# Two decoder layers on one core: which matmul a chain step, a norm's transposes and a broadcast are issued behind, and how eight PSUM banks are divided

## The chip, the cores and the metric

One core of one Trainium2 chip runs the whole program. The metric is device time in microseconds (us) of one execution; the median of the executions is compared. TensorE is PE in the profile, VectorE DVE, ScalarE ACT, GpSimd POOL and SyncE, which issues the weight loads, SP.

## What is computed

Two layers of a decoder trunk on 256 tokens of width 2048, in float32:

```python
for i in range(DEPTH):                                   # 2 layers
    h = h + mixers[i](rmsnorm(h, attn_norms[i]))         # 0: DeltaNet heads + latent attention, 1: retention
    h = h + conv_ffn(rmsnorm(h, ffn_norm), w_up, conv_w, conv_b, w_down)   # 2048 -> 2*5632 -> 2048
    h = h + (p[i] @ w_proj) * sigmoid(rmsnorm(h, gate_norm) @ w_gate)      # per-layer embedding (PLE)
return rmsnorm(h, final_norm)
```

In layer 0 the mixer projects the normed h with one 2048 x 5200 matrix. Eight gated DeltaNet heads get q, k, v and z from it. Each head needs a long chain of small products: normed keys, a triangular system solved by repeated products of 128 x 128 blocks, then the output. Eight latent-attention heads get low-rank queries and keys.

## The kernel before

**Projections.** Every weight is loaded from memory in pieces of up to 1 MB (`load`), and `split` makes of each piece a rounded part `hi` (a cast on ACT, L183) and a remainder `lo` (a subtraction on DVE, L184). Activations are kept in the same two parts. `gemm_b` computes 256 output columns transposed: for each half of the 2048 rows, sixteen `hi` matmuls of 512 columns (L239) and sixteen `lo` ones of 256 (L243). `gemm_a` computes up to 512 output columns for both halves of the tokens, with 8 + 8 `hi` matmuls (L265, L266) and 8 `lo` ones (L270) for each 512 rows of the weight. Both are Python generators: each `yield` is a place at which the program may put other work. `joined` reads a `gemm_b` result out of PSUM (ACT L249, DVE L250).

**Order of issue.** A scheduler goes through the program as it is written. On each engine it issues the earliest written instruction that its own model of the durations takes to be ready; the written order alone does not fix the order on PE. A NoSync edge (`tc.issue_after(x)`) keeps what is written in its block behind x on x's engine.

**The mixer of layer 0.** The heads go in four pairs. `Pair.solve` is the chain from the keys to the solved system `Ut`, `Pair.mix` the chain from there to the head's output, `masks` the decay factors that `solve` needs. Stage `step` of five runs `solve` of pair `step` and `mix` of pair `step - 1` in turns (`turns`). `weave(main, filler, rate)` writes `rate` pieces of filler after each step of a chain. The filler is the projections of the next heads (`gdn_gemm`) and the attention of one pair of heads (`mla`), alternating; in the last stage it is the output projection (`proj_add`). A piece of filler is some 1.4 to 1.9 us of matmuls, but four of the fifteen pieces of `mla` are empty. `unit_norm` transposes a head's keys or queries into a PSUM bank and returns that bank; it is read a second time after the norm is known (DVE L625 for k, L685 for q).

**Norms.** `Norm.feed(c)` transposes 512 columns of h on PE (`gained`, L285) and writes them in two parts (ACT L289, DVE L290). It is called as soon as `proj_add` has added its result to those columns (DVE L329). `Norm.finish` forms the factor of each token (DVE L311 and L312, a power on POOL in `rsqrt` L157) and, where it is asked to, turns it into a row with a diagonal (DVE L317), a matmul with ones (PE L319) and a copy (ACT L321). `low_rank` does the same for the low-rank queries and keys (DVE L481) and transposes at once.

**PSUM.** There are eight banks. Tiles `pa` take two banks, tiles `pb` one. The mixer of layer 0 has two `pa` and four `pb`; then this pool is closed and another with three `pa` and two `pb` opened for all that follows.

Of the kernel before, what the change touches and what calls it, by code (L numbers as in the profile page):

```python
# [29 lines left out]
PSUM0 = (2, 4)  # L30
PSUM1 = (3, 2)
NPART = 3
RATES = [2.0, 1.0, 1.0, 1.0, 2.5]
# [48 lines left out]
def trunk(ctx: ExitStack, tc: tile.TileContext, a: dict):  # L82
# [9 lines left out]
    banks = {}  # L92

    @contextmanager
    def psum(wide, narrow):

        with tc.tile_pool(name="psa", bufs=wide, space=PSUM) as banks["a"], tc.tile_pool(name="psb", bufs=narrow, space=PSUM) as banks["b"]:
            yield
# [17 lines left out]
    def pa():  # L116
        return banks["a"].tile([P, 2, 512], F32, tag="pa", name=nm("pa"))

    def pb():
        return banks["b"].tile([P, 512], F32, tag="pb", name=nm("pb"))  # L120
# [74 lines left out]

    def weave(main, filler, rate):
        owed = 0.0
        for _ in main:
            owed += rate
            while owed >= 1.0:  # L200
                owed -= 1.0
                next(filler, None)
        run(filler)
# [26 lines left out]
    def gemm_b(w, c0, tiles):  # L230
        ps = pa()
        for c in range(2):
            hi, lo = split(w[c * 1024 : (c + 1) * 1024, c0 : c0 + 256], 8, 256)
            for j in range(2):
                for k in range(8):
                    x2, xh = xr(tiles, c * 8 + k)
                    wh = hi[k][:, j * P : (j + 1) * P]
                    first = c == 0 and k == 0
                    T.matmul(ps[:, j], wh, x2, start=first, stop=False)  # L239
                yield  # L240
            for j in range(2):
                for k in range(8):
                    T.matmul(ps[:, j, :S], lo[k][:, j * P : (j + 1) * P], xr(tiles, c * 8 + k)[1], start=False, stop=c == 1 and k == 7)  # L243
# [11 lines left out]
    def gemm_a(w, r0, nkb, c0, n, tiles, ps=None, begin=True, end=True):  # L255
        if ps is None:
            ps = pa()
        k0 = 0
        while k0 < nkb:
            nk = min(4, nkb - k0)  # L260
            hi, lo = split(w[r0 + k0 * P : r0 + (k0 + nk) * P, c0 : c0 + n], nk, n)
            for i in range(NH):
                for k in range(nk):
                    xh, xw = xl(tiles, k0 + k, i)
                    T.matmul(ps[:, i, :n], xh, hi[k], start=begin and k0 + k == 0, stop=False)  # L265
                    T.matmul(ps[:, i, :n], xw, hi[k], start=False, stop=False)  # L266
                yield
            for i in range(NH):
                for k in range(nk):
                    T.matmul(ps[:, i, :n], xl(tiles, k0 + k, i)[0], lo[k], start=False, stop=end and k0 + k == nkb - 1)  # L270
# [23 lines left out]
    class Norm:  # L294
# [14 lines left out]
        def finish(self, bc):  # L309
# [5 lines left out]
            if bc:  # L315
                dg = t1((P, 2, P))
                V.tensor_tensor(dg, bcm(ident, 2), bcs(self.r, P), op=ALU.mult)  # L317
                ps = pb()
                T.matmul(ps[:, :S], ones, dg.rearrange("p a b -> p (a b)"), start=True, stop=True)  # L319
                self.bc = cp.tile([P, S], F32, name=nm("rbc"), tag="rbc")  # L320
                A.copy(self.bc, ps[:, :S])  # L321

    def proj_add(w, parts, cols, after=None):
        for c in cols:
# [5 lines left out]
            if after is not None:  # L330
                after(c)
# [44 lines left out]
    layer0 = ExitStack()  # L376
    layer0.enter_context(psum(*PSUM0))

# [18 lines left out]
    for c in range(CG):  # L397
        if c < CG - 2:
            for i in range(NH):
                load_x(i, c + 2)  # L400
        for _ in range(2):
            next(first_gemm)
        if c < CG - 1:
            n0.feed(c + 1)
        with tc.issue_after(last_gain[0].ins):
            Norm.squares(n0, c)
        next(first_gemm)
    n0.finish(True)
# [64 lines left out]
    def low_rank(src, gain):  # L473
# [8 lines left out]
        return gained(src, gain)  # L482

    for g3 in range(3):
# [7 lines left out]
        if g3 == 2:  # L492
            gates()
            cqT = low_rank(cq, C_QN)
# [88 lines left out]
    def unit_norm(f):  # L583
        ps = units(f)
        sq = t2((P, 4, P))
        A.activation(sq, v4(ps), AF.Square)
# [5 lines left out]
        return ps, rr  # L592

    class Pair:
# [27 lines left out]
        def solve(self):  # L622
            ps, rk = unit_norm(box.pop((self.hp, 1)))
            kh = self.kh = t2((P, 4, P))
            V.tensor_tensor(kh, v4(ps), bcs(rk, P), op=ALU.mult)  # L625
            yield from self.masks()
# [54 lines left out]
        def mix(self):  # L681
            hp, kh, kT, Ut = self.hp, self.kh, self.kT, self.Ut
            ps, rq = unit_norm(box.pop((hp, 0)))
            qh = t2((P, 4, P))
            V.scalar_tensor_tensor(qh, v4(ps), P ** -0.5, bcs(rq, P), op0=ALU.mult, op1=ALU.mult)  # L685
# [3 lines left out]
            V.tensor_tensor(vb, v4(ps), bcs(self.sc(beta), P), op=ALU.mult)  # L689
            yield  # L690
# [4 lines left out]
            ps = mm2(Ut, vb, first, first)  # L695
            u0 = t1((P, 2, P))
            A.copy(u0, two(ps))
            kd = t1((P, 2, P))
            V.tensor_tensor(kd, kh.rearrange("p (j i) d -> p i j d", i=2)[:, 0], bcs(kdx[:, 2 * hp : 2 * hp + 2, 0], P), op=ALU.mult)
# [5 lines left out]
            ps = mm2(kd, u0)  # L705
            S1 = t1((P, 2, P))
            A.copy(S1, two(ps))
# [4 lines left out]
            yield  # L712
            ps = mm2(kT, S1, second)
            r1 = t1((P, 2, P))
            for j in range(2):
                V.scalar_tensor_tensor(r1[:, j], ps[:, j * P : (j + 1) * P], nbe[:, 2 * hp + j, 1:2], vb[:, 2 * j + 1], op0=ALU.mult, op1=ALU.add)
# [24 lines left out]
            yield  # L741
            yield
# [89 lines left out]
    first_k = gdn_gemm(0, 1, box)  # L832
    for _ in range(2):
        next(first_k)
    ckvT = low_rank(ckv, C_KVN)
    next(first_k)
    make_kp()
    run(first_k)
    for step in range(5):
        chains = []  # L840
        if step < 4:
            chains.append(pairs[step].solve())
# [11 lines left out]
        if step == 0:  # L854
            for _ in range(3):
# [6 lines left out]
    n.finish(True)  # L862
    layer0.close()
    ctx.enter_context(psum(*PSUM1))


    def ffn(l, nf, nxt, aside=None):
# [33 lines left out]
        for g0, g1 in groups:  # L901
# [7 lines left out]
            prev = (g0, g1, cur)  # L909
        run(proj_add(w_dn, [(prev[0] * P, prev[2], prev[1] - prev[0])], range(CG), nxt.feed))  # L910
        nxt.finish(False)
        return ple_tiles(pin[0])
# [16 lines left out]
    def ple_add(i, c, ps, psp, r):  # L929
        sg = t2()  # L930
        A.activation(sg, ps[:, i], AF.Sigmoid, scale=r[:, i : i + 1])
# [305 lines left out]
```

## Time and profile before

| | us |
|---|---|
| median of 3 runs | 2927.84 (2927.80 to 2928.09) |
| profiled execution, its own time | 2927.71 |
| profiled execution, span from first to last instruction | 2925.9 |
| mean granted TensorE clock, share of full speed | 0.998 |

The span is the stretch which every view of the trace covers; the other 1.8 us lie around it. "Busy" is the time in which an engine executes at least one instruction. A matmul's end is modelled: a lone one of 512 columns is shown as 0.39 us long although the next may start 0.23 us after it, so that a pause between matmuls shows some 0.17 us shorter as idle time than it is between starts.

### The profile page before, as it was taken

The numbers are of one execution on the slowest core, as the hardware profiler recorded it, in microseconds if no ns is written. First come the engines' busy times: TensorE is split into PE (matmuls) and PEld (weight loads), VectorE is DVE, ScalarE is ACT, GpSimd is POOL, SyncE is SP. The second block draws the span as 40 slices with busy tenths as digits, with TensorE's granted clock in tenths as the row PEclk, the third lists the DMA queues.
The fourth block names the chain that finished last, engine by engine and source line by source line (L and its number), as shares of the span: only waits on it lengthen the run. The fifth ranks groups of instructions, "written<-read, shape, count | busy, mean of one in ns | idle before, by whom it ended". The sixth has DMA issues, their size and how long they took to land.

```text
span 2925.9 us, 38285 instructions
## 1 busy us (share of the span) xinstructions
PE 2891.1 (99%) x15172; PEld 2481.1 (85%) x15172; DVE 1932.5 (66%) x2705; ACT 1457.6 (50%) x2090; POOL 63.4 (2%) x68
## 2 busy tenths in 40 slices
PE   9999999999999999999999999999999999999998
PEld 8888887888888888888888888888888888888887
DVE  7877766776676767656556565565677767666665
ACT  7655554555454545554444444444554545445454
POOL 0111100000000000000000000000000000000000
PEclk9999999999999999999999999999999999999999
DMA  7434354555555555555555555555555555555554
GB/s 239 129 128 127 112 173 158 187 187 192 197 187 188 191 199 191 180 187 183 181 184 176 191 186 189 186 180 187 177 190 195 188 187 189 196 194 187 196 175 161
DMA packets 391973, 528.91 MB, mean 181 GB/s; under 512 B 9072, under 2 KB 265200, under 8 KB 391792
## 3 DMA queue, kind: packets, MB, share of 16 engines
q1 hardware_dynamic: 388656, 522.07, 54.1%
q10 hardware_dynamic: 3136, 4.38, 0.5%
q8 instruction: 119, 1.95, 0.3%
q14 instruction: 62, 0.51, 0.1%
HBM read 524.32 MB, written 2.10 MB: 180 GB/s over the span
## 4 chain that ended last, share of the span: by engine, by line
PE 93%; DVE 3%; issue 1%; ACT 1%; POOL 1%; DMA 0%; SPq 0%; POOLq 0%; ACTq 0%; DVEq 0%
PE pa L239 28%; PE pa L243 15%; PE pa L266 14%; PE pa L265 14%; PE pa L270 14%; PE pb L565 1%; DVE lo L184 1%; PE pb L285 1%; POOL small L157 1%; ACT hi L183 1%; PE pa L986 0%; PE pb L761 0%; PE pb L571 0%; DMA raw<-in_l_w_out_dram 0%; PE pb L1086 0%
## 5 line engine op out<-in xcount | busy, mean ns | idle before, releaser
L184 DVE TENSOR_TENSOR lo<-raw,hi 128x1024 fp32r<-128x1024 f32 (+3 forms) x1133 | 1203.5, 1082 | 673.2 <-ACT hi L183 624.8
L183 ACT CAST hi<-raw 128x1024 fp32r<-128x1024 f32 (+3 forms) x1133 | 1014.6, 935 | 1104.2 <-PE pa L266 496.1
L239 PE MATMUL pa<-xg,hi 128*128 128x512 f32 x3840 | 930.1, 393 | 0.5 <-ACT rbc L321 0.5
L239 PEld LDWEIGHTS pa<-xg,hi 128*128 128x128 f32 x3840 | 705.8, 189 | 136.9 <-ACT rbc L321 1.2
L266 PE MATMUL pa<-hi,xg 128*128 128x512 f32 (+1 forms) x1952 | 757.2, 388 | 0.0
L265 PE MATMUL pa<-hi,xg 128*128 128x512 f32 (+1 forms) x1952 | 756.1, 387 | 0.0
L243 PEld LDWEIGHTS pa<-xg,lo 128*128 128x128 f32 x3840 | 491.3, 191 | 17.0
L243 PE MATMUL pa<-xg,lo 128*128 128x256 f32 x3840 | 502.6, 283 | 0.0
L270 PE MATMUL pa<-lo,xg 128*128 128x512 f32 (+1 forms) x1952 | 481.5, 387 | 0.0
L266 PEld LDWEIGHTS pa<-hi,xg 128*128 128x128 f32 x1952 | 366.6, 188 | 70.9
L265 PEld LDWEIGHTS pa<-hi,xg 128*128 128x128 f32 x1952 | 366.6, 188 | 70.6
L270 PEld LDWEIGHTS pa<-lo,xg 128*128 128x128 f32 x1952 | 363.6, 188 | 71.6
L885 DVE SCALAR_TENSOR_TENSOR t<-t,fp,t 128x255 f32<-128x255 f32 x352 | 161.8, 480 | 111.8 <-ACT t L883 108.6
L249 ACT COPY t<-pa 128x512 f32<-128x512 f32 x120 | 70.5, 588 | 70.6 <-PE pa L243 69.8
L883 ACT ACTIVATE t<-t,fp 128x256 f32<-128x256 f32 x176 | 95.7, 591 | 0.0
L329 DVE TENSOR_TENSOR t<-t,pa 128x512 f32<-128x512 f32 x142 | 91.0, 680 | 3.8 <-PE pa L270 3.8
L157 POOL TENSOR_TENSOR small<-small,mhalf 128x1 f32<-128x1 f32 (+2 forms) x38 | 30.3, 797 | 2764.6 <-DVE small L312 1712.1
L250 DVE TENSOR_TENSOR t<-t,pa 128x512 f32<-128x512 f32 x120 | 81.6, 680 | 6.1 <-ACT t L249 6.1
L290 DVE SCALAR_TENSOR_TENSOR xg<-pb,par,xg 128x256 fp32r<-128x256 f32 x136 | 59.9, 479 | 34.7 <-ACT xg L289 33.0
L252 DVE TENSOR_TENSOR t<-t,rbc 128x512 f32<-128x512 f32 x104 | 71.0, 683 | 0.2
L894 ACT ACTIVATE t<-t 128x512 f32<-128x512 f32 x44 | 27.9, 633 | 70.8 <-DVE t L885 70.8
L289 ACT ACTIVATE xg<-pb,par 128x256 fp32r<-128x256 f32 x136 | 57.7, 470 | 7.6 <-PE pb L285 4.8
(233 smaller groups left out, 1205.5 us busy)
## 6 DMA issues: line engine op xcount, KB each, us to landing
raw<-in_l_ffn_w_up_dram SPq DMA_DIRECT2D x176, 1024.0 KB, 5.1
raw<-in_l_w_in_dram SPq DMA_DIRECT2D x128, 1024.0 KB, 5.0
raw<-in_l_ffn_w_down_dram SPq DMA_DIRECT2D x88, 1024.0 KB, 5.1
raw<-in_l_w_out_dram SPq DMA_DIRECT2D x44, 1024.0 KB, 5.2
raw<-in_l_ple_gate_dram SPq DMA_DIRECT2D x32, 1024.0 KB, 5.2
raw<-in_l_w_in_dram SPq DMA_DIRECT2D x11, 736.0 KB, 5.6
t<-in_x_dram SPq DMA_DIRECT2D x16, 256.0 KB, 6.0
raw<-in_l_mla_w_ukv_dram SPq DMA_DIRECT2D x4, 1024.0 KB, 5.1
```

What stands on the lines that cost most here:

```text
L183: A.copy(vo(hi)[:, c], vi(rk)[:, c])
L184: V.tensor_sub(vo(lo)[:, c], vi(rk)[:, c], vo(hi)[:, c].bitcast(F32))
L239: T.matmul(ps[:, j], wh, x2, start=first, stop=False)
L243: T.matmul(ps[:, j, :S], lo[k][:, j * P : (j + 1) * P], xr(tiles, c * 8 + k)[1], start=False, stop=c == 1 and k == 7)
L250: V.tensor_add(u, u, ps[:, :, :S])
L252: V.tensor_tensor(u, u, bcm(r, 2), op=ALU.mult)
L265: T.matmul(ps[:, i, :n], xh, hi[k], start=begin and k0 + k == 0, stop=False)
L266: T.matmul(ps[:, i, :n], xw, hi[k], start=False, stop=False)
L270: T.matmul(ps[:, i, :n], xl(tiles, k0 + k, i)[0], lo[k], start=False, stop=end and k0 + k == nkb - 1)
L329: V.tensor_add(h[i][c], h[i][c], ps[:, i])
L883: A.activation(y[:, j], u[:, j], AF.Identity, scale=fc(ct + 176), bias=fc(ct + 264))
L885: V.scalar_tensor_tensor(y[:, j, lag:], u[:, j, : S - lag], fc(ct + (2 - lag) * 88), y[:, j, lag:], op0=ALU.mult, op1=ALU.add)
```

## The change

- `last_mm` holds the latest matmul written by `gemm_a` or `gemm_b`. `behind(step)` writes a step with its PE instructions queued behind that matmul. `later(...)` puts steps in a list, and `turn()`, called by both generators after each block of matmuls, writes the first one of the list behind the block.
- `weave` writes the fillers first and then a chain step behind them; the rates change.
- Norm feeds, `finish`, diagonal, broadcast, the transposes of the low-rank tensors, the PLE input and the retention heads' tails go through `later` or `behind`. `finish` is split in three.
- `unit_norm` copies the transposed head out of PSUM and works on the copy. `masks` of a pair are written at the end of the preceding pair's `solve` (the first ones during the first key projection) and no longer inside `solve`.
- In `mix` some steps change places and one more empty step stands ahead of the last transposes. The first stage is given five pieces of filler ahead of its chain in place of three.
- PSUM is two `pa` and four `pb` for the whole program. Retention scores and outputs and the PLE projection use `pb`.

```diff
-PSUM0 = (2, 4)
-PSUM1 = (3, 2)
+PSA = 2
+PSB = 4
-RATES = [2.0, 1.0, 1.0, 1.0, 2.5]
+RATES = [1.8, 1.15, 1.15, 1.0, 2.3]
...
+    def behind(step):
+        with tc.issue_after(last_mm[0].ins):
+            return step()
+    def later(*steps):
+        todo.extend(steps)
+    def turn():
+        if todo:
+            behind(todo.popleft())
     def weave(main, filler, rate):
         owed = 0.0
-        for _ in main:
+        while True:
             owed += rate
             while owed >= 1.0:
                 owed -= 1.0
                 next(filler, None)
+            if behind(lambda: next(main, main)) is main:
+                break
         run(filler)
...
             for i in range(NH):
                 for k in range(nk):
...
+                    last_mm[0] = T.matmul(o[i], xw, hi[k], start=False, stop=False)
+                turn()
                 yield
...
+        def close(self):
+            later(self.finish, self.diagonal, self.broadcast)
...
             if after is not None:
-                after(c)
+                later(partial(after, c))
...
-        for _ in range(2):
+        next(first_gemm)
+        if c < CG - 1:
+            behind(partial(n0.feed, c + 1))
+        for _ in range(2):
             next(first_gemm)
-        if c < CG - 1:
-            n0.feed(c + 1)
...
-    n0.finish(True)
+    n0.finish()
+    n0.diagonal()
+    later(n0.broadcast)
...
-            cqT = low_rank(cq, C_QN)
+            low_rank(cq)
+            cqT = []
+            later(lambda: None, lambda: None, lambda: cqT.extend(gained(cq, C_QN)))
...
     def unit_norm(f):
         ps = units(f)
+        raw = t2((P, 4, P))
+        A.copy(raw, v4(ps))
         sq = t2((P, 4, P))
-        A.activation(sq, v4(ps), AF.Square)
+        A.activation(sq, raw, AF.Square)
...
-            ps, rk = unit_norm(box.pop((self.hp, 1)))
-            kh = self.kh = t2((P, 4, P))
-            V.tensor_tensor(kh, v4(ps), bcs(rk, P), op=ALU.mult)
-            yield from self.masks()
+            kh, rk = unit_norm(box.pop((self.hp, 1)))
+            self.kh = kh
+            V.tensor_tensor(kh, kh, bcs(rk, P), op=ALU.mult)
+            yield
             yield
...
-            yield
-            yield
+            for _ in range(3):
+                yield
             ps = unT(o)
...
+    next(first_k)
+    low_rank(ckv)
+    first_mask = pairs[0].masks()
+    next(first_mask)
     for _ in range(2):
         next(first_k)
-    ckvT = low_rank(ckv, C_KVN)
+    behind(make_kp)
     next(first_k)
-    make_kp()
+    ckvT = behind(lambda: gained(ckv, C_KVN))
+    next(first_k)
+    behind(lambda: run(first_mask))
     run(first_k)
     for step in range(5):
         chains = []
         if step < 4:
-            chains.append(pairs[step].solve())
+            solve = [pairs[step].solve()]
+            if step < 3:
+                solve.append(pairs[step + 1].masks())
+            chains.append(chain(*solve))
...
-            for _ in range(3):
+            for _ in range(5):
                 next(filler)
...
-    n.finish(True)
-    layer0.close()
-    ctx.enter_context(psum(*PSUM1))
+    n.close()
...
-            nxt.feed(c)
-        nxt.finish(True)
+            later(lambda: None, partial(nxt.feed, c))
+        nxt.close()
```

## Rows read from the trace of the kernel before

**Rows 1.** The page: busy time, share of the span and instructions of each engine; and the chain of work that ended last, by engine.

```profile
PE 2891.1 (99%) x15172; PEld 2481.1 (85%) x15172; DVE 1932.5 (66%) x2705; ACT 1457.6 (50%) x2090; POOL 63.4 (2%) x68
PE 93%; DVE 3%; issue 1%; ACT 1%; POOL 1%; DMA 0%; SPq 0%; POOLq 0%; ACTq 0%; DVEq 0%
```

**Rows 2.** Busy time by stretch: the stretch from and to in us, its length, then busy us (instructions) of PE, PE's weight loads, DVE, ACT and POOL, granted clock, DMA share and GB/s. The second stage of the mixer, its end with the start of the feed-forward block, and the feed-forward block of layer 0.

```profile
143.00:228.00 85.00, 81.42 (x534) 72.69 (x533) 64.26 (x127) 50.17 (x103) 11.76 (x9) 1.00 0.38 122
...
462.00:508.00 46.00, 41.26 (x183) 32.41 (x182) 32.83 (x57) 24.71 (x47) 0.70 (x1) 0.93 0.54 178
508.00:1190.00 682.00, 682.00 (x3665) 591.98 (x3664) 471.61 (x605) 342.20 (x426) 0.00 (x0) 1.00 0.58 190
```

**Rows 3.** The waits of PE over the whole span: the waiting line, what it waited for, us in total, how often, the longest.

```profile
PE pb L559 <- DVE t L676: 4.5, 3, 1.6
PE pb L613 <- ACT t L609: 3.7, 4, 1.0
PE pb L319 <- DVE t L317: 3.2, 2, 2.6
PE pb L761 <- DVE t L685: 2.4, 3, 0.8
PE pb L285 <- DVE t L329: 1.9, 4, 0.8
PE pb L285 <- DMA t<-in_x_dram: 1.4, 2, 1.1
PE pb L553 <- ACT t L547: 1.4, 1, 1.4
PE pb L285 <- DVE t L481: 1.3, 2, 0.7
...
PE pb L565 <- DVE t L638: 1.0, 3, 0.3
PE pb L319 <- DVE xg L290: 0.9, 2, 0.6
```

**Rows 4.** The instructions in order of time in the feed-forward block: start, us, engine, line, operation, output and inputs, how many in a row, idle time before them and what ended it. One projection ends, its bank is read, the next one runs.

```profile
559.69 3.82 PE L239 MATMUL pa<-xg,hi 128*128 128x512 f32 x16
559.89 0.59 ACT L249 COPY t<-pa 128x512 f32<-128x512 f32 x1 [0.26 <-PE pa L243]
560.56 0.68 DVE L250 TENSOR_TENSOR t<-t,pa 128x512 f32<-128x512 f32 x1
...
563.35 2.08 PE L243 MATMUL pa<-xg,lo 128*128 128x256 f32 x16
...
570.83 3.82 PE L239 MATMUL pa<-xg,hi 128*128 128x512 f32 x16
```

**Rows 5.** PE's instructions in order of time in the second stage of the mixer: three of its pauses.

```profile
159.08 1.54 PE L239 MATMUL pa<-xg,hi 128*128 128x512 f32 x6
161.52 0.50 PE L613 MATMUL pb<-t,triu_r 128*128 128x512 f32 x1 [0.90 <-ACT t L609]
...
162.94 1.55 PE L243 MATMUL pa<-xg,lo 128*128 128x256 f32 x11
165.28 1.19 PE L761 MATMUL pb<-xg,hi 128*128 128x512 f32 x4 [0.80 <-DVE t L685]
...
174.20 0.80 PE L763 MATMUL pb<-xg,lo 128*128 128x256 f32 x2
175.32 1.13 PE L565 MATMUL pb<-t,t 128*128 128x128 f32 x8 [0.33 <-DVE t L638]
```

**Rows 6.** The instructions in order of time where the mixer of layer 0 ends and the feed-forward block starts.

```profile
494.12 1.07 PE L270 MATMUL pa<-lo,xg 128*128 128x512 f32 x4
...
495.23 1.28 DVE L329 TENSOR_TENSOR t<-t,pa 128x512 f32<-128x512 f32 x2 [1.32 <-PE pa L270]
...
495.97 0.44 PE L285 MATMUL pb<-ident,t 128*128 128x128 f32 x2 [0.78 <-DVE t L329]
...
500.08 1.19 PE L319 MATMUL pb<-t,ones 128*128 128x256 f32 x2 [2.64 <-DVE t L317]
...
501.74 6.12 PE L239 MATMUL pa<-xg,hi 128*128 128x512 f32 x16 [0.46 <-ACT rbc L321]
...
507.69 2.07 PE L243 MATMUL pa<-xg,lo 128*128 128x256 f32 x16
```

**Rows 7.** Busy time by stretch, as in rows 2, of the sixteen matmuls that start at 501.74.

```profile
502.00:507.60 5.60, 5.60 (x16) 4.42 (x17) 4.32 (x12) 0.59 (x1) 0.00 (x0) 0.60 0.02 5
```

**Rows 8.** A copy of a whole PSUM bank by ACT, from the groups by line: us busy, mean ns of one, idle before.

```profile
L644 ACT COPY t<-pb 128x512 f32<-128x512 f32 x4 | 2.4, 588 | 4.4 <-DVE t L642 4.4
```

**Rows 9.** PE's instructions in order of time at the end of the stage of rows 5: the fourth pause.

```profile
213.22 2.08 PE L239 MATMUL pa<-xg,hi 128*128 128x512 f32 x8
215.13 0.60 PE L559 MATMUL pb<-ident,t 128*128 128x128 f32 x4
217.16 0.66 PE L559 MATMUL pb<-ident,t 128*128 128x128 f32 x4 [1.42 <-DVE t L676]
```

**Rows 10.** A DVE product of two SBUF tensors beside a POOL product, and the same line with no POOL product beside it; in order of time, DVE, POOL, DVE.

```profile
212.22 1.76 DVE L740 TENSOR_TENSOR t<-t,small 128x512 f32<-128x512 f32 x1 [0.90 <-POOL small L157]
...
212.16 1.27 POOL L662 TENSOR_TENSOR t<-t,cst 128x512 f32<-128x512 f32 x1
...
451.19 0.69 DVE L740 TENSOR_TENSOR t<-t,small 128x512 f32<-128x512 f32 x1 [1.12 <-POOL small L157]
```

## What is predicted

> **What bounds the kernel now.** I read the page first. PE is busy for 99% of the span and makes up 93% of the chain that ended last [rows 1], so only what PE does counts, and a change that takes no matmul away can win no more than PE's pauses. The next question is where these lie. Busy time by stretch answers it: in the feed-forward block of layer 0 PE is busy for all of 682 us, in one stage of the mixer it misses 3.6 of 85, and where the mixer ends 4.7 of 46 [rows 2]. The list of PE's waits then names the steps, all of them on `pb` banks: chain steps (L559, L613, L565, L553), norm transposes (L285), broadcasts (L319) and the attention's projections (L761) [rows 3]. They add up to some 22 us. No wait on a weight part, L183 or L184, is among these.
>
> Two scales are needed. At full pace sixteen `hi` matmuls take 563.35 - 559.69 = 3.66 us, 0.229 each [rows 4], and eleven `lo` ones at 0.119 take 1.31. A pause costs more than its idle time shows, because a matmul's modelled end hides the start of it: six `hi` matmuls from 159.08 should have ended at 160.45 and the next instruction starts at 161.52, so 1.07 us are lost where 0.90 are shown as idle [rows 5]. I add 0.17 us for each wait.
>
> **The seam to the feed-forward block.** From 494.12 to 507.69 PE needs 13.57 us for 4 `lo` matmuls of 512 columns (0.91), 8 transposes (0.11 each, 0.87), two broadcast halves (0.32) and 16 `hi` matmuls (3.66), in all 5.76 [rows 4, 6]: 7.8 us are lost. The rows give the order: PE waits for the add to h, then for the diagonal, then for the copy of the broadcast, since the first projection's bank belongs to a pool that can open only when the old one is empty. The sixteen matmuls after that run at a granted clock of 0.60, most of the time at 1.2 GHz in place of 2.4, after PE had done next to nothing for 6 us [rows 6, 7]. With the change there is no pool to wait for: the next projection starts at once, the last feed stands behind its first eight matmuls, finish, diagonal and broadcast behind later blocks, and the row is wanted only when a whole projection of 11.14 us has ended [rows 4]. What is late next is the last feed: eight matmuls cover 1.8 us, the two adds end 1.5 us after the last matmul if DVE is free [rows 6]; a piece of `lo` in front of them would add 1.2. I leave 0.6 (0 to 0.9) as a rest and the clock stays up. Saved: 7.2 us.
>
> **The other seams.** Diagonal and broadcast elsewhere: L319 waits 3.2 - 2.64 + 0.9 = 1.46 us in three places [rows 3, 6], with 0.17 each 2.0. Low-rank transposes, L285 behind L481: 1.3 + 0.3 = 1.6 [rows 3]. They now stand one to three blocks (1.4 us or more each) later, behind work that is there. Of the feeds' waits behind L329 0.8 belong to the seam above, some 0.7 lie in the last, short columns of the output projection, where nothing more can stand between, and the rest, 0.4, is in the PLE layers. I take 0.5 with its hidden part. Saved: 4.1 us.
>
> **The decay masks.** L613 waits for L609 four times, 3.7 us, lost 4.4 [rows 3]. Today the masks are written between `solve`'s first steps; two casts and two DVE products later PE wants them. They move to the end of the stage before, where the attention's pieces are used up and two full pieces of projection, 3.7 us, stand between cast and use. Saved: 4.4, at least 2.5.
>
> **The bank that is given back earlier.** L761 is the attention's own projection. It depends on nothing of `mix`, yet waits for L685: the four `pb` are taken, one by `unit_norm`, whose second reader comes after square, reduction and power. The copy frees that bank after 0.59 us on ACT [rows 8]. Three waits, 2.4 us, lost 2.9 [rows 3]. Saved: 2.9. The price is eight copies, 4.7 us on an ACT that is busy for 50 of 85 us [rows 2]; the chain has four steps of time for them, so nothing on PE. Without that cover it would be 0.6 each.
>
> **The last doubling step.** At 217.16 the transposes of `Ut` wait 1.42 us for L676, three times, 4.5, lost 5.0 [rows 3, 9]. Between the product and these transposes stand eight `hi` matmuls, the output's transposes and an empty piece, 2.3 us in all; 3.9 were needed. By my count of pieces at rate 1.15 (33 steps, 38 pieces) the attention has run out there, and two full pieces, 3.7 us, stand between. Saved: 1.3 of 1.6 each time, 4.1 (0 to 5.0).
>
> **The first key.** L553 waits 1.4 us once, lost 1.6 [rows 3]; one more full piece stands in front of it than before. Saved: 1.4.
>
> **What stays, and what could come.** L565 behind L638 (174.20 to 175.32: 0.9 us lost each time [rows 5]) keeps its two pieces of cover and stays: 0 (0 to 2.6). At the higher rate the attention's empty pieces fall between other steps, which then have one block and a short step of cover, 2.1 us; steps with just that cover don't wait today. I charge 1.5 (0 to 4). At the start the transposes of the second columns no longer hold up the first matmuls until x has landed: up to 1.4 gained [rows 3], or as much lost if weights and x are late; I take 0. Two `pa` after the mixer: 0, see below.
>
> There is one more price. The norm's product reads the copy in SBUF where it read PSUM. L740 has two SBUF inputs: it takes 0.69 us alone and 1.76 beside a POOL product [rows 10]; eight such collisions would be 8.6 us on DVE. I take 0: POOL's mask products leave that place with the change, and the doubling products come later.
>
> The Trainium skill, SBUF — State Buffer, section "Who interferes with whom", says that a VectorE instruction with two SBUF inputs and a GpSimd instruction that reads SBUF lock each other out, and that the later one waits for the whole of the other. The trace agrees: L740 starts 0.06 us after a POOL product of 1.27 us and takes 1.07 us longer than alone. By that rule the changed product can collide and the old one could not, which speaks against this part of the change.
>
> **Sum.** 7.2 + 4.1 + 4.4 + 2.9 + 4.1 + 1.4 - 1.5 = 22.6 us. The profiled execution took 2927.71, 0.13 from the median: 2905.1, taken as 2905, 0.8% faster.
>
> **Rivals.** *The chain waits somewhere else.* The results that PE waits for come from DVE and ACT queues which the change doesn't shorten (DVE 64 of 85 us [rows 2]); a step set later in one place takes the cover of the next. Then only the seams are saved, 7.2 + 4.1: 2916. For it: DVE's share, and L565. Against it: three of the four pauses of a stage are a late mask, a held bank and an empty piece. 13%.
>
> *Every pause goes*, the rests above too (1.5 + 0.6 + 0.9 + 0.2 + 2.6 + 0.9 = 6.7, and 1.4 at the start): 2897. 6%.
>
> *The copied norm collides with POOL*, and PE waits for each: 22.6 - 8.6 = 14.0, 2914. 3%.
>
> *Slower: two `pa` are too few.* From the feed-forward block on, a projection may start only when the one two before it has been read out. That takes until 561.24, 1.6 us after the bank's last matmul; the next projection lasts to 570.83 [rows 4]. So it decides only if reading starts over 9 us late. If 120 transposed projections (L250's count) each waited 0.4 us, 48 us are lost and 22.6 won: 2953. The rows speak against it. 3%.
>
> *The ties do nothing*: an edge only keeps a step from coming too early, and the seams stay as they were because the scheduler issues the feeds in the same places: within 5 us of today, 2924. Against it: the closed pool. 4%.
>
> **Range and chances.** The forecast has 71%, with its own range 2899 to 2912. The range 2897 to 2916 reaches to "every pause goes" and to "seams only". Faster or slower than 0.2%, 5.9 us, is about what a measurement of this kernel tells from no change. Faster: 71 + 13 + 6 + 3, less a little of the second for its edge near 2922: 0.91. Same: 0.05. Slower: 0.04.
>
> **What would show it.** Right: in the list of PE's waits L613, L761 and L553 are gone or under 0.5 us, L559 behind L676 under 1.5, no L319 over 0.3; at the seam the `hi` matmuls follow the last `lo` ones at 0.229 us with clock 1.00; L565 behind L638 still there; feed-forward blocks as long as before. Wrong: new chain lines with a microsecond or more each in that list; `hi` matmuls waiting for L250 or L329; a granted clock below 1 in any stretch where it was 1.

## The result and the profile after

The changed kernel takes 2907.74 us (2906.75 to 2908.33) beside 2927.85 for the kernel before: 20.1 us less, a ratio of 0.993 with an interval of 0.991 to 0.995. The forecast was 2905, its likeliest case 2899 to 2912. The profiled execution took 2907.72 with a span of 2905.8.

Busy time and the chain that ended last, by engine, of the kernel after; the lines answer to [rows 1].

```profile
PE 2883.8 (99%) x15172; PEld 2483.2 (85%) x15172; DVE 1935.0 (67%) x2697; ACT 1459.0 (50%) x2097; POOL 62.0 (2%) x68
PE 95%; DVE 2%; ACT 1%; DMA 1%; issue 0%; POOL 0%; POOLq 0%; ACTq 0%; DVEq 0%
```

PE has the same 15172 matmuls. Of the 20 us, 13 are idle time of PE that is gone. Its busy time falls by 7 us: in it lie the hidden parts of the pauses and matmuls that no longer run at the low clock. PE's waits after, to set beside [rows 3] (line that waited, what it waited for, us in total, times, longest):

```profile
PE pa L282 <- ACT xg L359: 2.6, 1, 2.6
PE pb L789 <- DVE lo L181: 2.5, 4, 0.8
PE pa L282 <- ACT hi L180: 1.5, 1, 1.5
PE pb L590 <- ACT t L699: 1.2, 1, 1.2
PE pb L404 <- POOL mhalf L146: 1.0, 1, 1.0
PE pb L590 <- DVE t L703: 0.8, 1, 0.8
PE pb L590 <- DVE t L669: 0.5, 1, 0.5
PE pa L283 <- DVE xg L309: 0.4, 2, 0.3
PE pb L590 <- DVE t L665: 0.4, 1, 0.4
PE pb L304 <- DVE t L505: 0.4, 1, 0.4
```

Every line of [rows 3] is gone or small: no mask matmul, attention projection (L787 now), doubling transpose (L584 now), first-key transpose (L578 now) or broadcast (L341 now) waits. In the stage whose rate stays at 1.0 the last doubling step still waits, at one of its products (L590 behind L699, 1.2 us). What else waits was not in [rows 3]: a `gemm_a` matmul for the split of a column of h (L359) and for a weight cast (L180), attention matmuls for a weight remainder (L181), chain products (L590).

The times between the first matmuls of the parts, from the two timelines, say where the 20 us come from. The last column adds up the terms of the prediction that lie in that part.

| part | before | after | change | foretold |
|---|---|---|---|---|
| start to the second group of the input projection | 27.79 | 29.99 | +2.2 | 0 |
| to the first matmul of stage 0 (low-rank transposes, one broadcast) | 49.55 | 48.15 | -1.4 | -2.4 |
| stage 0 (first key, one mask) | 77.96 | 77.77 | -0.2 | -2.5 |
| stages 1 to 3 (three masks, bank, doubling step, the charge of 1.5) | 242.13 | 229.60 | -12.5 | -8.8 |
| last stage and output projection up to its last column | 74.75 | 78.66 | +3.9 | 0 |
| last column to the second half of the first feed-forward projection | 37.42 | 29.59 | -7.8 | -7.2 |
| the rest | 2405.49 | 2401.30 | -4.2 | -1.7 |

(In the sixth row the broadcast, 0.43 us of PE, stands later after the change and is counted in it all the same.) Of the 2.0 us that the prediction has for three broadcasts, 0.8 belong to the second row, by this line of the kernel before:

```profile
28.73 0.67 PE L319 MATMUL pb<-t,ones 128*128 128x256 f32 x2 [0.61 <-DVE t L317]
```

Some work also changes rows. The first pair's mask matmuls, 0.5 us, now stand in the second row and stage 3 has none; four key transposes, 0.4 us, have gone from the end of stage 0 into stage 1, and four from stage 3 into the last stage. So stage 0 has in truth gained nothing.

The total is right because misses of both signs cancel: 6.1 us are lost in two places for which the prediction had no loss, 2.3 fewer than foretold are won in stage 0, and on balance 6 more in the other rows.

**The seam** went as foretold. PE's instructions after, where the mixer ends, answering to [rows 6]:

```profile
485.98 1.07 PE L288 MATMUL pa<-lo,xg 128*128 128x512 f32 x4
486.89 1.98 PE L253 MATMUL pa<-xg,hi 128*128 128x512 f32 x8
488.71 1.04 PE L304 MATMUL pb<-ident,t 128*128 128x128 f32 x8
489.50 2.09 PE L253 MATMUL pa<-xg,hi 128*128 128x512 f32 x8
491.43 2.07 PE L258 MATMUL pa<-xg,lo 128*128 128x256 f32 x16
493.34 2.00 PE L253 MATMUL pa<-xg,hi 128*128 128x512 f32 x8
495.18 0.59 PE L341 MATMUL pb<-t,ones 128*128 128x256 f32 x2
```

The first `hi` matmul starts 0.91 us after the last four `lo` ones, where 7.62 lay between (494.12 to 501.74 in [rows 6]). Transposes and broadcast stand between blocks and wait for nothing, and eight `hi` matmuls take 1.8 us, at a granted clock of 1.00.

**The start** lost 2.2 us. ACT and PE after, in the first columns:

```profile
13.74 0.83 ACT L308 ACTIVATE xg<-pb,par 128x256 fp32r<-128x256 f32 x2
...
14.46 0.63 ACT L326 ACTIVATE t<-t 128x512 f32<-128x512 f32 x1
...
15.69 1.69 ACT L180 CAST hi<-raw 128x368 fp32r<-128x368 f32 x4
...
16.23 0.44 PE L282 MATMUL pa<-hi,xg 128*128 128x368 f32 x1 [1.48 <-ACT hi L180]
```

The feed of the next columns is tied behind eight matmuls. Its copies (L308) and the squares (L326) come later than they could and stand in ACT's queue ahead of the weight casts, and PE waits for the first of these.

**The last stage** lost 3.9 us, its low clock in the first column after it included. The instructions in order of time after, where the last head's output joins the output projection:

```profile
446.91 0.60 PE L584 MATMUL pb<-ident,t 128*128 128x128 f32 x4
...
450.39 1.04 ACT L180 CAST hi<-raw 128x1024 fp32r<-128x1024 f32 x1 [3.54 <-DMA raw<-in_l_w_out_dram]
451.34 0.61 ACT L359 CAST xg<-t 128x512 fp32r<-128x512 f32 x1
...
452.01 0.73 PE L282 MATMUL pa<-hi,xg 128*128 128x512 f32 x2 [2.65 <-ACT xg L359]
```

Busy time by stretch, as in [rows 2], before and after that wait:

```profile
444.00:449.20 5.20, 5.20 (x26) 4.11 (x24) 3.02 (x3) 1.63 (x2) 0.00 (x0) 1.00 0.80 271
...
452.00:457.00 5.00, 4.99 (x14) 3.69 (x15) 1.81 (x2) 1.04 (x1) 0.00 (x0) 0.66 0.54 202
```

The last transposes of the chain (L584) come so late that eight matmuls are left behind them, 1.9 us from 447.27 on. The cast of the head's output (L359) stands in ACT's queue behind a weight cast that waits for its DMA. PE pauses for 2.65 us, and the matmuls that follow run at a granted clock of 0.66: partly at 1.2 GHz, where it was 2.4 before the pause. That costs 5.0 x 0.34 = 1.7 us more.

### The profile page after: what moved, and what is told of

It is laid out like the page before. It is cut to its first block, busy times and chain, and to the rows that moved or that the text cites. A ratio compares the mean times of both kernels' runs of the same rounds, so it can differ in the third digit from the quotient of the medians.

```text
span 2905.8 us, 38267 instructions
## 1 busy us (share of the span) xinstructions
PE 2883.8 (99%) x15172; PEld 2483.2 (85%) x15172; DVE 1935.0 (67%) x2697; ACT 1459.0 (50%) x2097; POOL 62.0 (2%) x68
## 4 chain that ended last, share of the span: by engine, by line
PE 95%; DVE 2%; ACT 1%; DMA 1%; issue 0%; POOL 0%; POOLq 0%; ACTq 0%; DVEq 0%
PE pa L253 29%; PE pa L258 15%; PE pa L282 15%; PE pa L283 15%; PE pa L288 15%; PE pb L590 2%; PE pb L304 1%; DVE lo L181 1%; PE pb L1023 0%; PE pb L596 0%; PE pb L234 0%; PE pb L232 0%; PE pb L231 0%; DMA raw<-in_l_w_out_dram 0%; DMA raw<-in_l_w_in_dram 0%
## 5 line engine op out<-in xcount | busy, mean ns | idle before, releaser
L181 DVE TENSOR_TENSOR lo<-raw,hi 128x1024 fp32r<-128x1024 f32 (+3 forms) x1133 | 1199.5, 1080 | 678.2 <-ACT hi L180 608.8
L180 ACT CAST hi<-raw 128x1024 fp32r<-128x1024 f32 (+3 forms) x1133 | 1015.1, 935 | 1082.9 <-PE pa L283 505.2
L282 PE MATMUL pa<-hi,xg 128*128 128x512 f32 (+1 forms) x1924 | 747.1, 388 | 4.2 <-ACT xg L359 2.6
L283 PE MATMUL pa<-hi,xg 128*128 128x512 f32 (+1 forms) x1924 | 745.6, 388 | 0.4 <-DVE xg L309 0.4
L288 PE MATMUL pa<-lo,xg 128*128 128x512 f32 (+1 forms) x1924 | 474.1, 387 | 0.0
L282 PEld LDWEIGHTS pa<-hi,xg 128*128 128x128 f32 x1924 | 361.4, 188 | 75.0 <-ACT xg L359 3.1
L283 PEld LDWEIGHTS pa<-hi,xg 128*128 128x128 f32 x1924 | 361.8, 188 | 71.6 <-DVE xg L309 0.9
L266 DVE TENSOR_TENSOR t<-t,pa 128x512 f32<-128x512 f32 x120 | 81.6, 680 | 0.3 <-ACT t L265 0.3
L308 ACT ACTIVATE xg<-pb,par 128x256 fp32r<-128x256 f32 x136 | 57.8, 468 | 9.4 <-PE pb L304 5.4
```

The lines of the kernel that those rows point to most:

```text
L180: A.copy(vo(hi)[:, c], vi(rk)[:, c])
L181: V.tensor_sub(vo(lo)[:, c], vi(rk)[:, c], vo(hi)[:, c].bitcast(F32))
L266: V.tensor_add(u, u, ps[:, :, :S])
L282: T.matmul(o[i], xh, hi[k], start=begin and k0 + k == 0, stop=False)
L283: last_mm[0] = T.matmul(o[i], xw, hi[k], start=False, stop=False)
L288: last_mm[0] = T.matmul(o[i], xl(tiles, k0 + k, i)[0], lo[k], start=False, stop=end and k0 + k == nkb - 1)
```

## The experiments

Except where it says "kernel before", an experiment edits the changed kernel. The kernel before, run beside the experiments, took 2926.87 to 2927.87 us in the three groups of runs, so a difference of under 1 us between kernels of different groups says nothing; the starts of the parts in the traces are firmer.

**The first columns without the tie.** The old order of the start, nothing else.

```diff
-        next(first_gemm)
-        if c < CG - 1:
-            behind(partial(n0.feed, c + 1))
         for _ in range(2):
             next(first_gemm)
+        if c < CG - 1:
+            n0.feed(c + 1)
...
+        next(first_gemm)
```

> The changed kernel with the four norm feeds of the start written as before: two blocks of matmuls, the feed with no tie, then the third block. Theory (the tie costs the start): in the changed kernel the feed of the second columns stands behind eight matmuls, its copies and the squares then hold back the casts of the second weight piece on ACT, and PE reaches the second projection's first matmul at 29.99 us where the kernel before reached it at 27.79. Untied, that mark is back under 28.3 and the whole about 2 us shorter, 2905 to 2906. Rival (the first weights and x merely landed later in that execution): the mark stays within 0.4 us of 29.99 and the time at 2907 to 2908.

Measured: 2905.94 us (2905.81 to 2906.32), 1.8 less than with the tie. The second group of the input projection starts at 28.00 in place of 29.99, and the last matmul of the program 1.8 us earlier. The tie is the cause of the loss at the start.

**The last stage's chain earlier.**

```diff
-RATES = [1.8, 1.15, 1.15, 1.0, 2.3]
+RATES = [1.8, 1.15, 1.15, 1.0, 1.8]
```

> The changed kernel with 1.8 pieces of output projection after each step of the last stage's chain in place of 2.3, so that the chain's last step stands after 27 of 36 pieces and no longer after 34. Theory (the chain ends too late): the wait of the output projection for the last head's cast, 2.65 us, and the slow matmuls behind it (eight at 0.2 us over pace, 1.6 us) go; 2903 to 2904. Rival (the cast is late because ACT stands in front of a weight cast that waits for its DMA, wherever the chain is): a wait of more than 1.5 us at the same line stays, 2906 to 2908. If steps that come closer together wait for each other, new waits of the chain's lines appear in this stage, up to 3 us.

Measured: 2903.49 us (2903.37 to 2904.38), 4.25 less. The last stage without the late columns takes 63.7 us, as in the kernel before (66.5 in the changed one), the wait for L359 is gone, and this is the one wait of PE from 384 to 490 us:

```profile
PE pb L304 <- DVE t L354: 0.8, 1, 0.8
```

So the loss in the last stage is a matter of how much filler is left when the chain ends, and mending it gives all of it back.

**Both mended** (the two edits above together).

> The changed kernel with both of its losses mended: the first columns untied as in the first of these runs, and 1.8 pieces per step in the last stage as in the second. The two lie 400 us apart, so the gains should add: 1.8 and 4.3 us off 2907.7, 2901 to 2902.5. If the end of the last stage depends on what the start left behind, 2903 to 2905.

Measured: 2902.58 us (2902.03 to 2902.99), a ratio of 0.991 to the kernel before (0.990 to 0.993). The gains are 1.8 and 4.25 alone and 5.2 together; they nearly add.

**The seam's norm written at once**, with the one PSUM layout kept.

```diff
-    run(proj_add(w_o, late, range(NPART), n.feed))
-    run(proj_add(w_o, early + late, range(NPART, CG), n.feed))
-    n.close()
+    run(proj_add(w_o, late, range(NPART), n.feed, True))
+    run(proj_add(w_o, early + late, range(NPART, CG), n.feed, True))
+    n.finish()
+    n.diagonal()
+    n.broadcast()
```

(With `True` as its last argument `proj_add` calls the feed at once.)

> The changed kernel with the norm at the seam to the feed-forward block written at once, as in the kernel before (feeds, finish, diagonal, broadcast right where they arise, nothing put off), but with the one PSUM layout kept. It tells the two parts of the seam apart. Theory A (the closing pool was the gate): the projection goes ahead while the norm is formed, at most 2.5 us of the 7.8 come back, the clock stays at 1.00, 2908 to 2910. Theory B (putting the norm off is what saves): the broadcast stands in front of the projection on PE, 5 to 8 us come back with the low clock, 2913 to 2916.

Measured: 2907.95 us (2907.87 to 2908.04), as long as the changed kernel. From the last column's start to the feed-forward block it is 22.70 us, as with the deferred steps (22.71) and unlike the kernel before (29.55).

**The kernel before with one PSUM layout**: the two double and four single banks throughout, with the readers of the second layout adapted as in the change; every norm is written at once as before.

```diff
-    layer0.enter_context(psum(*PSUM0))
+    ctx.enter_context(psum(*PSUM0))
...
-    n.finish(True)
-    layer0.close()
-    ctx.enter_context(psum(*PSUM1))
+    n.finish(True)
```

> The kernel before, with one part of the change: one PSUM layout of two double and four single banks throughout, every norm still written at once. If the closing pool alone made the pause ahead of the feed-forward block: the step from the last output column to the block is 22.7 us in place of 29.6, the clock stays up, 7 to 9 us in all: 2919 to 2921. Rival: in the old order the block's first projection stands behind the norm's broadcast on TensorE anyway, and half of the pause or more stays: 2924 or more.

Measured: 2920.60 us (2920.32 to 2920.99) beside 2927.22: 6.6 less, ratio 0.9977 (0.9967 to 0.9987). PE's instructions at the seam (its L238 is the `hi` matmul, L285 the transposes):

```profile
494.10 1.07 PE L270 MATMUL pa<-lo,xg 128*128 128x512 f32 x4
495.01 1.07 PE L238 MATMUL pa<-xg,hi 128*128 128x512 f32 x4
495.95 0.44 PE L285 MATMUL pb<-ident,t 128*128 128x128 f32 x2
496.14 0.72 PE L238 MATMUL pa<-xg,hi 128*128 128x512 f32 x2
...
500.13 0.67 PE L319 MATMUL pb<-t,ones 128*128 128x256 f32 x2 [0.31 <-DVE t L317]
```

The matmuls start 0.91 us after the last `lo` ones although the norm is written ahead of them: the scheduler takes them first as soon as they have a bank. By the same marks as in the table the seam takes 30.35 us in place of 37.42. The granted clock from 494 to 503 us is 1.00. Both runs together show that the closing of the pool made the pause, and that writing the steps later adds 0.8 us at most.

**No ties at all.**

```diff
     def behind(step):
-        with tc.issue_after(last_mm[0].ins):
-            return step()
+        return step()
```

> The changed kernel with the same written order, but no edge anywhere behind a stated matmul. Theory (the written order and the freed resources save, the edges are bounds that seldom bind): 2906 to 2909.5, each middle stage within 0.8 us of 79.9. Rival (the edges are what keeps a step from being issued before its input is there): the middle stages are 2 to 4 us longer each, 2914 to 2920.

Measured: 2905.48 us (2904.62 to 2906.75), 2.3 less than with the ties. Stages 1 to 3 take 79.90, 79.87 and 69.86 us, with ties 79.89, 79.87 and 69.84, and the start gains what the first experiment gained (28.05). The edges of the change bring nothing in stages 1 to 3. What gains is the order in which the steps are written, with the layout and the rates. Not all of the 2.3 us need be a gain of this edit: two of the four executions took 2904.6 us and two 2906.3 and 2906.8, and in the traced one, of 2904.62, PE still waits 2.55 us in the last stage, but its clock stays at 1.00 after it, which is worth 1.7 us.

**The masks back inside the solve.** The second step of `solve` runs its own pair's masks, as in the kernel before; the copy of the norm and all else stay.

```diff
-            yield
+            yield from self.masks()
...
-            if step < 3:
-                solve.append(pairs[step + 1].masks())
```

> The changed kernel with the decay masks back between the first steps of the solving chain. Theory (their place was the cause of the waits for the cast): four waits of the cumulative product for its cast return, about 1 us each, 4.4 us in all, 2911 to 2913. Rival (the closer filler covers them wherever they stand): no such wait over 0.3 us, 2907 to 2909.

Measured: 2915.71 us (2913.02 to 2917.86), 8.0 more. Stages 0 to 3 are longer by 0.4, 3.7, 2.2 and 3.0 us. But the mask matmul itself waits for only 0.6 us:

```profile
PE pb L536 <- DVE t L795: 6.4, 3, 2.4
...
PE pb L640 <- ACT t L636: 0.6, 1, 0.6
```

L536 is the attention's rotary product; L795 adds the two parts of the heads that it reads. Instructions of the second stage in order of time:

```profile
161.96 1.04 POOL L645 TENSOR_TENSOR t<-cst,beta 128x512 f32<-128x512 f32 x1
162.02 1.52 DVE L652 TENSOR_TENSOR t<-t,small 128x512 f32<-128x512 f32 x1 [0.90 <-POOL small L154]
...
167.94 4.08 DVE L181 TENSOR_TENSOR lo<-raw,hi 128x512 fp32r<-128x512 f32 x5
...
171.94 0.41 DVE L795 TENSOR_TENSOR t<-t,pb 128x256 f32<-128x256 f32 x1
...
172.40 0.70 PE L536 MATMUL pb<-t,cst 128*128 128x256 f32 x2 [2.44 <-DVE t L795]
...
172.75 1.84 PE L787 MATMUL pb<-xg,hi 128*128 128x512 f32 x4
```

Busy time by stretch, from that product on:

```profile
172.40:176.40 4.00, 4.00 (x16) 3.62 (x17) 3.26 (x7) 0.37 (x1) 0.00 (x0) 0.60 0.98 304
```

DVE is late: the norm's product (L652) meets POOL's mask product and takes 1.52 us (0.69 with the masks moved, at 162.88 in the changed kernel), the mask products follow, five weight remainders stand in front of the addition L795, and PE pauses for 2.44 us and goes on at a granted clock of 0.60, four attention matmuls taking 1.84 us instead of 1.18. Some 1.7 us of the 3.7 in stage 1 are this low clock; in stage 2 a wait as long, 2.43 us at 255.95, left the clock at 1.00. The executions of this kernel lie 4.8 us apart, so that 8.0 is a rough figure.

**The kernel before with the masks moved**: the first pair's stay in its `solve`, the others are written at the end of the stage before.

```diff
-            yield from self.masks()
+            if self.hp == 0:
+                yield from self.masks()
+            else:
+                yield
...
-            chains.append(pairs[step].solve())
+            solve = [pairs[step].solve()]
+            if step < 3:
+                solve.append(pairs[step + 1].masks())
+            chains.append(chain(*solve))
```

> The kernel before, with one part of the change: the decay masks of stages 1 to 3 are written at the end of the stage before, and only the first pair's stay inside the solve. My prediction's term by itself: three of four mask pauses go, 3.3 us: 2924.6, with the attention's wait behind the norm's reduction as before (2.4 us). Rival, from the run with the masks put back: the masks hold up the whole VectorE queue, so that the attention's wait and others shrink with them: 2921 or less, 2.0 us or more less in each of stages 1 to 3.

Measured: 2921.58 us (2920.98 to 2922.75) beside 2927.22: 5.6 less, ratio 0.998 (0.997 to 0.999). Stages 1 to 3 are shorter by 2.5, 1.8 and 2.5 us, stage 0, which now ends with the next pair's masks, is 1.3 longer. This lies near the rival: more goes than the three mask pauses. The waits that remain, of those in [rows 3]:

```profile
PE pb L559 <- DVE t L679: 4.3, 3, 1.4
...
PE pb L613 <- ACT t L609: 1.0, 1, 1.0
```

The wait of the attention's projection (L761 behind L685 in [rows 3], 2.4 us) is gone, without any copy. PE's second attention projection and DVE's second read of the norm's bank, in the second stage (L764 and L688 are L761 and L685 of the kernel before):

```profile
162.77 1.17 PE L764 MATMUL pb<-xg,hi 128*128 128x512 f32 x4
...
164.40 0.69 DVE L688 SCALAR_TENSOR_TENSOR t<-pb,small 128x512 f32<-128x512 f32 x1 [1.12 <-PE pb L766]
```

The projection runs 1.6 us before the norm's bank is read for the last time. So four banks are enough with that bank held. By this the fifth claim on them was that of the masks: in the kernel before their matmul takes a bank at 161.52 [rows 5], and ACT reads it only at 165.61:

```profile
165.61 0.60 ACT L616 ACTIVATE t<-pb 128x512 f32<-128x512 f32 x1
```

The move also takes the masks' products out of DVE's queue at that place; no run separates the bank from the queue.

**The changed kernel without the copy of the norm**: `unit_norm` returns the PSUM bank again.

```diff
-        raw = t2((P, 4, P))
-        A.copy(raw, v4(ps))
         sq = t2((P, 4, P))
-        A.activation(sq, raw, AF.Square)
+        A.activation(sq, v4(ps), AF.Square)
...
-        return raw, rr
+        return ps, rr
```

> The changed kernel with the old unit_norm: no copy out of PSUM, the bank is read a second time after the norm's factor is known. Theory (the held bank was what the attention's projection waited for): waits of the attention's matmuls for the product of queries and factor return in the three middle stages, about 1 us each, 2910 to 2912. Rival (with the steps spread over the stage the four banks suffice): the middle stages stay at 79.9 us within 0.4, the whole at 2907 to 2908.5.

Measured: 2906.04 us (2905.77 to 2906.16), 1.7 less. Stages 1 to 3 are 0.4 us shorter each, stage 0 by 0.25, and no wait on the norm's bank appears. In the changed order the copy is only a price.

**The kernel before with the copy of the norm**, the same edit the other way round.

> The kernel before, with one part of the change: the unit norm copies its PSUM bank to SBUF first. My prediction: the bank was what the attention waited for, its wait behind the reduction (2.4 us shown) goes, 2.9 us are saved: 2925.0. Rival: the attention would wait for the next bank or for the key anyway, and the copy stands in ScalarE's queue ahead of others: 2927.5 to 2930, the wait gone under that name, new ones in its place.

Measured: 2930.39 us (2928.84 to 2931.60) beside 2927.22: 3.2 more, ratio 1.001 (1.000 to 1.002). The attention's wait for a bank is gone. One of its later projections now waits for a weight remainder (L764 here is the `lo` matmul), and DVE's products of SBUF tensors meet POOL's. One of PE's waits, then instructions of the second stage:

```profile
PE pb L764 <- DVE lo L184: 5.1, 4, 1.6
```

```profile
160.68 1.03 POOL L620 TENSOR_TENSOR t<-cst,beta 128x512 f32<-128x512 f32 x1
160.74 1.52 DVE L627 TENSOR_TENSOR t<-t,small 128x512 f32<-128x512 f32 x1 [0.90 <-POOL small L157]
...
174.36 0.38 PE L764 MATMUL pb<-xg,lo 128*128 128x256 f32 x1 [1.64 <-DVE lo L184]
```

Busy time by stretch after this wait in stages 1 to 3, each time 1.64 us long:

```profile
174.40:178.40 4.00, 3.55 (x19) 2.78 (x20) 3.41 (x8) 1.06 (x3) 0.00 (x0) 1.00 0.18 35
258.70:263.70 5.00, 4.67 (x18) 3.90 (x19) 3.46 (x8) 1.21 (x3) 0.00 (x0) 0.66 0.36 92
344.20:349.20 5.00, 4.68 (x18) 3.93 (x19) 3.47 (x8) 1.05 (x3) 0.00 (x0) 0.66 0.34 94
```

The rival held. In that order the copy frees a bank earlier, but PE then waits for a weight remainder from the late DVE queue: it starts the projection 1.9 us earlier (171.22 in place of 173.08), and DVE ends the remainder only 0.25 us earlier. So stage 1 is no shorter, 84.30 us in place of 84.36. Stages 2 and 3 are 1.2 and 1.0 us longer, and there the clock falls after the wait, 5.0 x 0.34 = 1.7 us each time. In the traced execution the copy's loss is this low clock.

**The middle rates back at 1.**

```diff
-RATES = [1.8, 1.15, 1.15, 1.0, 2.3]
+RATES = [1.8, 1.0, 1.0, 1.0, 2.3]
```

> The changed kernel with one piece of filler after each step in the second and third stage in place of 1.15. Theory (an empty piece of attention in front of the last doubling step was the cause of its wait): the transposes of the solved system, or the product beside them, wait for the last subtraction again, 1.0 to 1.6 us in each of the two stages, 2909.5 to 2911. Rival (the output's extra empty step and the shorter DVE queue removed it): both stages stay at 79.9 us within 0.4, 2907 to 2908.5.

Measured: 2911.02 us (2910.48 to 2911.10), 3.3 more; stages 1 and 2 take 81.6 and 81.7 us, 1.7 and 1.8 more. The pause is at the last doubling step, though not at the transposes of `Ut` but at the product that follows the copy L699:

```profile
PE pb L590 <- ACT t L699: 3.9, 3, 1.4
```

**All that helped, together**: no ties, 1.8 in the last stage, no copy of the norm.

> Three edits that each made the changed kernel faster, in one kernel: no step is tied behind a matmul (2905.5 alone), the last stage's rate is 1.8 (2903.5 alone), and the unit norm reads the PSUM bank with no copy (2906.0 alone). If they act in different places (the start; the last stage; stages 1 to 3) their gains of 2.3, 4.3 and 1.7 us add up: 2899.5, within 2898.5 and 2901. Rival: the order of the steps shifts with each of them and the copy is needed where the rate changes: 2902 or more, no better than with the start and the last stage alone (2902.6).

Measured: 2902.44 us (2902.13 to 2902.53), ratio 0.992 (0.990 to 0.993). This is no better than the two mended places alone (2902.58), as the rival said. Stages 1 to 3 gain their 0.4 us each (79.50, 79.50 and 69.46), and the last stage gives it back (64.67 in place of 63.69). Which of the edits does that was not separated.

## Why the prediction was right, and where not

*Seam, 7.2:* right in mechanism, 7.8 in size; the rest of 0.6 us that I left for the last feed did not appear. The layout alone saves 6.6 us of the whole time, so the closed pool was the gate; that finish, diagonal and broadcast are written later is worth under 1 us here. The clock stays at its high level because the pause is gone.

*Other seams, 4.1:* the waits went as foretold, the sum is too small. Up to stage 0 it is 1.4 (2.4 foretold), or 1.9 without the mask matmuls that now stand there; after the seam 4.2 (1.7 foretold). By the starts of the same projections 2.4 of the 4.2 lie between 1213 and 1417 us of the kernel before (the end of the first feed-forward block, its PLE layer, the start of retention). The waits of PE in the whole rest add up to only 1.2 us in the kernel before, the layout alone gives 0.3 there, and without the ties the rest is as long to 0.1 us. Where the surplus of 2.5 comes from is not shown.

*Masks, 4.4:* the part was the right one, its mechanism too narrow. I priced the mask matmul's own wait. Moving the masks alone saves 5.6 us in the old order and 8.0 in the changed one, because they also held a fourth bank for 4 us and put products into a DVE queue that is already late (how much is due to each was not separated). The step that failed is "two casts and two DVE products later PE wants them": others behind them in the queue are wanted too.

*Bank given back earlier, 2.9:* wrong. The wait that the term was read from did go, but it goes without the copy too, once the masks have moved. The copy costs 1.7 us in the changed order (1.4 of it in stages 0 to 3), and 3.2 in the old, where PE waits for a weight remainder instead and its clock falls after two of three such waits. The failed step is the inference from a releaser's name: L685 was the last reader to let go of a bank, not the reader whose bank had to be freed, and PE's next input was late as well.

*Last doubling step, 4.1:* right in cause, but in two stages only; 3.3 to 3.6 in size by the rates put back. The term counts three stages (and three times 1.3 is 3.9), but in stage 3 the rate stays at 1.0, and 1.2 us of its pause stay too, at L590 behind L699.

*First key, 1.4, and one mask in stage 0:* both waits went, but the stage gained 0.2 us, not 2.5, and nothing when the four key transposes that left it are counted. There the rival "the chain waits somewhere else" holds: 1.6 for weight remainders, 0.8 and 0.5 for chain products (L703, L669). The charge of 1.5 for such waits was too small for this stage and not needed in stages 1 and 2. The wait that I let stay (L565 behind L638, three times) also went almost wholly, 0.4 us once.

*Start, taken as 0:* it lost 2.2. I had bounded it at 1.4 by the transposes' wait for x, and had not followed what the late feed does to ACT's queue, where its copies and squares stand ahead of the weight casts.

*Last stage:* the prediction has no term for it. The rate went from 2.5 to 2.3, but by my count of `mix`'s steps, now fifteen, the chain ended with two pieces of filler behind it where it had four (15 x 2.3 = 34 of 36 pieces ahead of its last transposes, 13 x 2.5 = 32 before). It cost 3.9 us, the largest single miss, and it shows a sign named under "wrong": a granted clock below 1 where it was 1. L590 behind L699 is another, a new chain line of over a microsecond.

*Copied norm against POOL, a rival at 3%:* it did not happen in the changed kernel, where L652 takes 0.69 us, but it is real: 1.52 us for the product of k in every stage of both runs in which copy and masks stood together (the product of q stays at 0.69). The Trainium skill, SBUF — State Buffer, section "Who interferes with whom", gives the rule for it, that the two engines share a pair of ports as an exclusive lock; both runs agree with it. The reason that I gave for taking 0, that the masks leave that place, is what the runs show.

*Two `pa` too few:* excluded. Sixteen `hi` and sixteen `lo` matmuls of the feed-forward block take 5.56 us from start to start before and after.

*The ties do nothing:* true of the ties, as the run without them shows, but not of the change, whose other parts make the gain. I had tied the time of that rival to the seam, which the layout mends without any tie.

## What to carry to other kernels

When an engine waits for a bank, list all holders of the pool and how long each keeps its bank; the releaser that the profile names is only the one that came last. Price a moved step by what stands behind it in every queue, above all in the queue that is already the latest. When a woven chain gets longer or its rate is changed, count the filler left behind its last step: the tail of the weave is where the cover runs out, and one constant there was worth 4 us.

## What the hardware showed

Much shorter pauses than the seam's six idle microseconds [rows 6, 7] brought PE's clock down, but not each time. After a wait of 2.44 us (the masks back in the solve, at 172.40) and one of 2.65 (the changed kernel, at 452.01) the next 5 us had a granted clock of 0.66, a mixture of the two levels, where it had been 1.00. After 2.43 us (the masks back in the solve, at 255.95) and 2.55 (no ties, at 450.52) it stayed at 1.00. The wait of 1.64 us in the kernel before with the copy left it at 1.00 in stage 1 and brought it to 0.66 in stages 2 and 3. So in these runs the length of the pause alone does not decide; what else does is not shown. Where the clock fell, it cost 5.0 x 0.34 = 1.7 us beyond the pause's length, which is about the distance between the two pairs of executions without ties.
